# Output projection as a stage of its own between attention and memory queries, by one level of Strassen's algorithm over pairs of token tiles

## Chip, cores and metric

The kernel runs as one program on one core of a Trainium2 chip. The metric is the device time of one execution in microseconds (us). The engines are TensorE (PE; matmuls, and PEld for its weight loads), VectorE (DVE), ScalarE (ACT), GpSimd (POOL) and SyncE (SP), whose queue issues most of the DMA transfers. GpSimd has a DMA queue of its own too (POOLq).

## What is computed

One layer of a streaming encoder over 2048 tokens of 1024 features:

```python
xn = rmsnorm(x, g_mix)
z = xn @ w_in                       # q, k, v (3 x 512), p_in (512), forget logits (8)
fox = forgetting_attention(q, k, v, f_logit)          # 8 heads of 64, causal, (S, 512)
pool = multiscale_pool(p_in, w_pool, pool_scale)      # windows 2, 4, 8, 16, (S, 512)
h = x + concatenate([fox, pool], -1) @ w_out          # w_out 1024 x 1024
mq = rmsnorm per head of (rmsnorm(h, g_mem_q) @ w_mem_q)   # 4 heads of 128
h = h + softmax(mq mk / sqrt(128)) mv @ w_mem_out     # 256 memory tokens
gu = rmsnorm(h, g_ffn) @ w_gate_up
h = h + (silu(gu[:, :2816]) * gu[:, 2816:]) @ w_down
```

All data is float32. A matmul of full precision is made as three in a reduced format (fp32r): each operand is split into a high part (a cast, usually on ScalarE: `act.copy`) and a low part (raw minus high, a subtraction `sub_hi` on VectorE or GpSimd), and `mm3` adds high·high, high·low and low·high into one PSUM bank. So each operand costs a cast and a subtraction, and each product three matmuls.

## The kernel before

Tokens are cut into 16 tiles of 128 (`NT`) or 8 blocks of 256 (`NB`). The stages follow one another on the time line of the profile: memory keys and values and the input projection (0 to 337 us), the pooling stage (337 to 541), the attention (541 to 953), the memory queries (953 to 1316), and the feed-forward part (1316 to 2588), which already uses Strassen's algorithm. TensorE runs in the order in which the program is written in all of these (`in_order`); in the pooling stage the other engines' order is the scheduler's, in the memory queries SyncE's is the program's too.

**Pooling stage.** A loop over blocks n. `project_p` (mm3 of x by the pool columns of the input weights) makes block n's projections in PSUM: 96 matmuls of 128x256, tile `zp`. `x_load`, `x_split` fetch and split a later block of x (raw and low parts take turns in nine places `xl`). `windows(n)` runs on VectorE: it scales out of PSUM into `pT`, makes window sums `s0` to `s3` by doubling, and `mixed`, and splits that into `mxh`, `mxl`. `pooled(n-1)` multiplies by `w_pool` (12 matmuls, tile `op`) and splits the result into `poh`, `pol`. `out_pool(n-2)` multiplies these by the lower 512 rows of `w_out` (`wop`, split on GpSimd at n = 0): 48 matmuls of 128x512 a block (tile `oo`), added to rows of x (`xr`) and written to `h1d`.

**Attention.** A software pipeline of scores and values over heads and blocks. Its result goes, transposed, to DRAM tiles `catT` of 512 tokens. In its tail the upper 512 rows of `w_out` (`wof`, by `load_w_of`) and `w_mem_q` (by `load_w_q`) are loaded and split.

**Memory queries.** A loop over 16 tiles, software-pipelined. `out_fox` multiplies a tile of `catT` (loaded by `load_cat`, split on VectorE) by `wof`, 24 matmuls of 128x512 a tile (tile `mmps`), and adds `h1d`. `query` takes the tile's norm and its transposes `hT`; `query_norm` multiplies by `w_mem_q` and norms each head (ScalarE twice, VectorE, GpSimd three times); `query_t` transposes; `softmax` makes 12 score matmuls of 128x256 (`scps`) and the exponentials; `mem_values` and `mem_out` follow some tiles later. Tiles 0 and 1 are projected ahead of the loop; in iterations n = 0 to 3 `out_fox(n+2)` stands where `mem_out` stands later, and from n = 4 on `out_fox(n+1)` stands between `query_norm` and `query_t`.

Of the kernel before, what the change touches and what calls it, by code (L numbers as in the profile page):

```python
# [16 lines left out]
P = 128  # L17
S = 2048
D = 1024
# [21 lines left out]
def block_kernel(ctx: ExitStack, tc: tile.TileContext, x, xT, memT, cols, rows, w_qkvf, w_p, w_pool, w_out,  # L41
# [9 lines left out]
    def f(ap):  # L51
        return ap.bitcast(F32)
# [54 lines left out]
    catT = [dr.tile([FOXW, 512], F32, name=f"catT{n}") for n in range(4)]  # L107
    h1d = [dr.tile([P, D], F32, name=f"h1d{n}") for n in range(NT)]
# [40 lines left out]
    def x_split(tiles, part=None, qs=range(4)):  # L149

        for q in qs:
# [9 lines left out]
            sub_hi(lo[:], raw[:], hi[:])  # L161
# [27 lines left out]
    with ExitStack() as c0:  # L189
# [120 lines left out]
        with ExitStack() as c1:  # L310
# [65 lines left out]
            def project_p(hs, ls, zs, ks):  # L376

                per = NG // len(zs)
                for k, g in ([(k, g) for k in ks for g in range(NG)] if per == 1 else
                             [(k, g) for g in range(NG) for k in ks]):  # L380
                    mm3(zs[g // per][:, g % per], (wph[k][:, g * P:(g + 1) * P], wpl[k][:, g * P:(g + 1) * P]),
                        (hs[k], ls[k]), k == 0, k == KD - 1)
# [81 lines left out]
    with xstack:  # L464
        wq_ = opened(xstack, "wo_pool", side="right")
# [13 lines left out]
        def stat_bcast(b):  # L479

            diag = xp.tile([P, 2, B], F32, tag="xsq", name="diag", bufs=2)[:, 0].rearrange("p (j t) -> p j t", j=2)
            for j in range(2):
                dve.tensor_scalar(out=diag[:, j], in0=ident[:], scalar1=rstd[:, 2 * b + j:2 * b + j + 1],
                                  scalar2=None, op0=ALU.mult)
            rbp = tpp.tile([P, B], F32, tag="ss", name="rb", bufs=1)
# [5 lines left out]
        def windows(b, zs, rb, prev):  # L491
# [6 lines left out]
            for i, z in enumerate(zs):  # L498
                dve.tensor_tensor(out=pT[:, per * i:per * i + per, HIS:], in0=z[:, :per],
                                  in1=rb.unsqueeze(1).to_broadcast([P, per, B]), op=ALU.mult)  # L500
            cur = pT
            mixed = pt.tile([P, NG, B], F32, tag="mixed", name="mixed")
            for st in range(NG):
                sh = 1 << st
                lead = 2 * sh - 1
                nx = pt.tile([P, NG, HIS + B], F32, tag=f"s{st % 2}", name=f"s{st}")
                dve.tensor_tensor(out=nx[:, st:, lead:], in0=cur[:, st:, lead:],
                                   in1=cur[:, st:, lead - sh:HIS + B - sh], op=ALU.add)
                dve.scalar_tensor_tensor(out=mixed[:, st], in0=nx[:, st, HIS:], scalar=1.0 / (2 * sh),
                                         in1=pT[:, st, HIS:], op0=ALU.mult, op1=ALU.subtract)  # L510
                if b == 0:
                    dve.tensor_tensor(out=mixed[:, st, :HIS], in0=nx[:, st, HIS:2 * HIS], in1=pinv[:, st],
                                      op=ALU.mult)
                    dve.tensor_tensor(out=mixed[:, st, :HIS], in0=mixed[:, st, :HIS], in1=pT[:, st, HIS:2 * HIS],
                                      op=ALU.subtract)
                cur = nx
            mxh = pt.tile([P, NG, B], F32R, tag="mxh", name="mxh")
            mxl = pt.tile([P, NG, B], F32R, tag="mxl", name="mxl")
            act.copy(mxh[:], mixed[:])
            sub_hi(mxl[:], mixed[:], mxh[:])  # L520
            return pT, mxh, mxl

        def pooled(mxh, mxl):
            poh = pt.tile([P, NG, B], F32R, tag="poh", name="poh")
            pol = pt.tile([P, NG, B], F32R, tag="pol", name="pol")
            for i in range(2):
                op = zpp.tile([P, 2, B], F32, tag="z", name="op", bufs=4)
                for j in range(2):
                    g = 2 * i + j
                    mm3(op[:, j], (wph2[:, g], wpl2[:, g]), (mxh[:, g], mxl[:, g]), True, True)  # L530
                for j in range(2):
                    g = 2 * i + j
                    split_gain(poh[:, g], pol[:, g], op[:, j], pscale[:, g:g + 1])
            return poh, pol

        def out_pool(b, poh, pol):
            for j in range(2):
                i = 2 * b + j
                ts = slice(j * P, (j + 1) * P)
                xr = pt.tile([P, D], F32, tag="xr", name="xr", bufs=4)  # L540
                sp.dma_start(xr[:], x[i * P:(i + 1) * P, :])
                for a in range(2):
                    ps = tpp.tile([P, 512], F32, tag="tp", name="oo", bufs=3)
                    for g in range(NG):
                        mm3(ps[:], (poh[:, g, ts], pol[:, g, ts]), (wop[g, a][0][:], wop[g, a][1][:]),
                            g == 0, g == NG - 1)
                    as_ = slice(a * 512, (a + 1) * 512)
                    dve.tensor_tensor(out=xr[:, as_], in0=ps[:], in1=xr[:, as_], op=ALU.add)
                pool.dma_start(h1d[i][:], xr[:])
# [34 lines left out]
        with in_order():  # L584
            prev, mxs, pos, cum = None, {}, {}, cumulated()
            for n in range(NB + 2):
                if n < NB:
                    hs, ls = nxt
                    if n == 0:
                        rb = stat_bcast(0)  # L590
                    else:
                        zs = [zpp.tile([P, 2, B], F32, tag="z", name="zp", bufs=4) for _ in range(2)]
                        project_p(hs, ls, zs, range(KD))
                    if n + 1 < NB:
                        if n > 0:
                            xt = x_load(n + 1)
                        x_split(xt)
                        nxt = x_parts(xt)
                    if n == 0:
                        wop = {}  # L600
                        for g in range(NG):
# [900 lines left out]
```

## Time and profile before

| | us |
|---|---|
| median of three runs | 2611.46 |
| lowest, highest | 2609.98, 2615.81 |
| the profiled execution | 2590.1 |
| its span in the trace | 2588.4 |
| TensorE busy in the span | 2539.1 (98%) |
| VectorE busy | 1700.5 (66%) |
| ScalarE busy | 1247.2 (48%) |
| GpSimd busy | 809.4 (31%) |

The profile is of one execution. Its page gives busy times, the span in 40 equal slices (64.7 us each; a digit is the busy share in tenths, PEclk the clock that TensorE was granted), and the chain of work that ended last. A row of the trace's time line gives start, duration, engine, line, operation, output and inputs, shape, and in brackets how long the engine had been idle before it and what released it. A matmul's duration is longer than the spacing of matmuls that follow one another, so the cost of one is read from starts. A group of instructions is given as busy time and mean ns of one, then the idle time before them and what ended it.

### The profile page before, as it was taken

The numbers are of one execution on the slowest core, as the hardware profiler recorded it, in microseconds if no ns is written. First come the engines' busy times: TensorE is split into PE (matmuls) and PEld (weight loads), VectorE is DVE, ScalarE is ACT, GpSimd is POOL, SyncE is SP. The second block draws the span as 40 slices with busy tenths as digits, with TensorE's granted clock in tenths as the row PEclk, the third lists the DMA queues.
The fourth block names the chain that finished last, engine by engine and source line by source line (L and its number), as shares of the span: only waits on it lengthen the run. The fifth ranks groups of instructions, "written<-read, shape, count | busy, mean of one in ns | idle before, by whom it ended". The sixth has DMA issues, their size and how long they took to land.

```text
span 2588.4 us, 36909 instructions
## 1 busy us (share of the span) xinstructions
PE 2539.1 (98%) x13133; PEld 2181.8 (84%) x13133; DVE 1700.5 (66%) x2933; ACT 1247.2 (48%) x2375; POOL 809.4 (31%) x1087
## 2 busy tenths in 40 slices
PE   8999999999999989999999999999999999999999
PEld 7999989878888868888778888888888888888887
DVE  6444475579889865445687778756766666664554
ACT  6454442158888864444543433334543333333443
POOL 3343230034444442333525455431001122222000
PEclk9999999999999999999999999999999999999999
DMA  6443475346446242222454554447773233334665
GB/s 242 126 133 104 127 221 167 134 134 148 106 119 152 54 134 91 86 86 82 159 207 166 196 187 170 164 159 254 254 268 131 94 125 107 108 116 163 235 208 203
DMA packets 217065, 396.20 MB, mean 153 GB/s; under 512 B 36656, under 2 KB 112176, under 8 KB 206128
## 3 DMA queue, kind: packets, MB, share of 16 engines
q1 hardware_dynamic: 187376, 296.30, 36.3%
q0 software_dynamic: 29504, 97.54, 9.7%
q8 instruction: 103, 1.69, 0.3%
q14 instruction: 82, 0.67, 0.1%
HBM read 268.85 MB, written 124.91 MB: 152 GB/s over the span
## 4 chain that ended last, share of the span: by engine, by line
PE 41%; issue 8%; DVE 1%; POOL 1%; ACT 0%; POOLq 0%; DVEq 0%
PE bk L62 13%; PE bk L60 13%; PE bk L61 13%; DVE ww L55 0%; POOL out_dram L1395 0%; PE mmps L60 0%; PE mmps L62 0%; PE mmps L61 0%; DVE t L966 0%; PE bk L934 0%; POOL xraw L906 0%; DVE cb L55 0%; ACT pm L1068 0%; DVE x22l L55 0%; ACT ww L178 0%
## 5 line engine op out<-in xcount | busy, mean ns | idle before, releaser
L55 DVE TENSOR_TENSOR ww<-draw,ww 128x512 fp32r<-128x512 f32 x308 | 204.4, 702 | 158.0 <-ACT ww L178 157.8
L178 ACT CAST ww<-draw 128x512 fp32r<-128x512 f32 x308 | 179.2, 620 | 221.8 <-PE bk L62 174.2
L55 DVE TENSOR_TENSOR ww<-graw,ww 128x512 fp32r<-128x512 f32 x220 | 178.3, 816 | 107.6 <-ACT ww L178 107.3
L61 PE MATMUL bk<-ww,ww 128*128 128x512 f32 x616 | 239.6, 389 | 0.0
L60 PE MATMUL bk<-ww,ww 128*128 128x512 f32 x616 | 239.6, 389 | 0.0
L62 PE MATMUL bk<-ww,ww 128*128 128x512 f32 x616 | 239.6, 389 | 0.0
L178 ACT CAST ww<-graw 128x512 fp32r<-128x512 f32 x220 | 136.0, 621 | 180.0 <-PE bk L62 160.1
L55 DVE TENSOR_TENSOR pl<-tp,ph 128x512 fp32r<-128x512 f32 (+3 forms) x296 | 176.7, 599 | 32.7 <-ACT ph L781 31.1
L765 PE MATMUL tp<-ident,s 128*128 128x128 f32 x1088 | 174.0, 276 | 8.1 <-DVE pl L55 7.8
L60 PE MATMUL zps<-wh,xhi 128*128 128x386 f32 x512 | 175.7, 343 | 0.1
L702 ACT ACTIVATE s<-s,mx 128x1024 f32<-128x1024 f32 (+2 forms) x192 | 173.8, 906 | 3.8 <-DVE mx L696 1.8
L61 PE MATMUL zps<-wl,xhi 128*128 128x386 f32 x512 | 173.6, 339 | 0.0
L62 PE MATMUL zps<-wh,xl 128*128 128x386 f32 x512 | 173.2, 338 | 0.0
L781 ACT CAST ph<-tp 128x512 fp32r<-128x512 f32 (+3 forms) x296 | 148.7, 514 | 38.8 <-PE tp L765 32.2
L765 PEld LDWEIGHTS tp<-ident,s 128*128 128x128 f32 x1088 | 134.8, 142 | 38.0 <-DVE pl L55 13.5
L750 PE MATMUL acc<-ph,v 128*128 128x512 f32 (+1 forms) x320 | 133.9, 422 | 6.0 <-POOL ph L770 4.9
L62 PE MATMUL bk<-qs,ww 128*128 128x512 f32 x352 | 137.2, 390 | 1.0 <-DVE ww L55 1.0
L60 PE MATMUL bk<-qs,ww 128*128 128x512 f32 x352 | 137.9, 392 | 0.3 <-ACT s L1314 0.3
L61 PE MATMUL bk<-kh,ww 128*128 128x512 f32 x352 | 137.0, 389 | 0.0
L60 PE MATMUL bk<-kl,ww 128*128 128x512 f32 x352 | 136.9, 389 | 0.0
L61 PE MATMUL bk<-cb,ww 128*128 128x512 f32 x352 | 136.9, 389 | 0.0
L62 PE MATMUL bk<-kl,ww 128*128 128x512 f32 x352 | 136.9, 389 | 0.0
(549 smaller groups left out, 7128.3 us busy)
## 6 DMA issues: line engine op xcount, KB each, us to landing
graw<-in_w_gu_dram SPq DMA_DIRECT2D x44, 1024.0 KB, 5.5
draw<-in_w_down_dram SPq DMA_DIRECT2D x66, 256.0 KB, 3.9
xl<-in_xT_dram SPq DMA_DIRECT2D x64, 256.0 KB, 4.8
qkT<-st SPq DMA_DIRECT2D x64, 256.0 KB, 2.7
wdr<-in_w_down_dram SPq DMA_DIRECT2D x22, 512.0 KB, 3.9
vd<-cb SPq DMA_DIRECT2D x16, 512.0 KB, 3.3
xr<-in_x_dram SPq DMA_DIRECT2D x16, 512.0 KB, 3.3
qs<-qkT SPq DMA_DIRECT2D x8, 1024.0 KB, 10.7
```

Source lines behind the costliest of these rows:

```text
L55: (eng or dve).tensor_tensor(out=lo, in0=src, in1=f(hi), op=ALU.subtract)
L60: pe.matmul(ps, lhsT=sh, rhs=mh, start=first, stop=False, skip_group_check=goes_on)
L61: pe.matmul(ps, lhsT=sh, rhs=ml, start=False, stop=False, skip_group_check=goes_on)
L62: pe.matmul(ps, lhsT=sl, rhs=mh, start=False, stop=last, skip_group_check=goes_on)
L178: act.copy(hi, raw)
L702: act.activation(s[:, sl], s[:, sl], AF.Exp, bias=ng, scale=-1.0, accum_out=l[:, q, g:g + 1])
L750: pe.matmul(acc[:, qa * P:], lhsT=v[:, j, :], rhs=pm[:, qa * P:], start=state["n"] == 1, stop=state["n"] == 2 * nk)
L765: pe.transpose(tp[:, q * P:(q + 1) * P], unit["rows"][q][:, j * P:(j + 1) * P], ident[:])
L781: act.copy(ph[:, sl], tp[:, sl])
```

## The change

The output projection is taken out of both stages and made one stage between the attention and the memory queries. For a pair of token tiles (i, i+4) the operand is a 2 by 2 matrix of blocks: x11 and x21 from the attention (`catT`), x12 and x22 from the pooling (now stored as `poolT`), each 128 tokens by 512 features; the weights are b11, b12, b21, b22, the quarters of `w_out`. The seven products of a pair are x11·b11, x12·b21, s2·t2, s1·t1, s3·t3, s4·b22 and x22·t4, where s1 = x21 + x22, s2 = s1 − x11, s3 = x11 − x21, s4 = x12 − s2 and t1 to t4 are sums of the weights. Sums of products gather in three PSUM banks and are added on VectorE to rows of x.

- Pooling stage: `out_pool` is gone. `pooled` scales its result into `po`, which GpSimd's queue writes to `poolT`. `out_sums` makes t1 to t4 from `w_out` (eight calls in all, each two loads of 256 KB, four subtractions of 128x256 on GpSimd, four writes of 128 KB on its queue). The last block's windows are made in two halves.
- Attention's tail: b11 and b21 are loaded and split in place of `wof`, t2 and t1 in place of `w_mem_q`, and the first pair's x11 and x12 are loaded and split.
- New stage: loop over eight pairs. Each loads four parts of 256 KB (the first pair two), makes two sums on VectorE and two on GpSimd, seven splits (ScalarE cast, VectorE subtraction), and 84 matmuls of 128x512; two products of a pair are made during the next. Operands take turns in eleven places. t3, t4 and b22 are loaded at the first pair, `w_mem_q` at the last. Queries 0 to 2, query_norm 0 and 1, and softmax 0 are made at its end.
- Memory queries: the loop starts at n = 2, without `out_fox`; `h1d` is loaded three tiles ahead; `hT` has three places; `w_mem_out` is loaded at the end of n = 2 and 3. `token_ops` subtractions go from GpSimd to VectorE.

```diff
             if n + 1 < NB:
                 if n > 0:
                     xt = x_load(n + 1)
-                x_split(xt)
+                x_split(xt, engs={} if n else {2: pool, 3: pool})
                 nxt = x_parts(xt)
-            if n == 0:
-                wop = {}
-                ...
-                        wop[g, a] = load_split(wq_, w_out[r0:r0 + P, a * 512:(a + 1) * 512], f"wop{g}{a}", pool)
+                diag = stat_diag(n + 1)
...
+            for k in {6: (4, 5), 7: (6, 7)}.get(n, (n - 2,)):
+                if k >= 0:
+                    out_sums(k // 2, k % 2)
-            prev, *mxs[n] = windows(n, zs, rb, prev)
+            prev, mxs[n] = windows(n, zs, rb, prev)
...
-        if n - 2 >= 0:
-            out_pool(n - 2, *pos.pop(n - 2))
-        if 0 <= n - 1 < NB:
-            pos[n - 1] = pooled(*mxs.pop(n - 1))
+        if n > 0:
+            for b in {1: (), 2: (0, 1)}.get(n, (n - 1,)):
+                pooled(b, mxs.pop(b))
...
+def out_sums(k, a):
+    raw = pt.tile([P, 4, B], F32, tag="wor", name="wor", bufs=2)
+    cs = slice(a * B, (a + 1) * B)
+    for c in range(2):
+        r0 = c * FOXW + k * P
+        sp.dma_start(raw[:, 2 * c:2 * c + 2], w_out[r0:r0 + P, :].rearrange("p (a c) -> p a c", a=2)[:, :, cs])
+    b11, b12, b21, b22 = (raw[:, n] for n in range(4))
+    t3 = pt.tile([P, B], F32, tag="wot", name="wot", bufs=2)
+    sub = lambda o, p_, q_: pool.tensor_tensor(out=o, in0=p_, in1=q_, op=ALU.subtract)
+    sub(t3[:], b22, b12)
+    sub(b12, b12, b11)
+    sub(b22, b22, b12)
+    sub(b21, b21, b22)
+    for nm, v in (("t3", t3[:]), ("t1", b12), ("t2", b22), ("t4", b21)):
+        pool.dma_start(osum[nm][:, k, cs], v)
...
+def pair_ops(p_, parts, raw):
+    ...
+    put("x22", x22)
+    tt(x22, x21, x22, ALU.add)
+    tt(x21, x11, x21, ALU.subtract, pool)
+    tt(raw[0], x22, x11, ALU.subtract)
+    put("s2", raw[0])
+    put("s1", x22)
+    put("s3", x21)
+    tt(raw[1], x12, raw[0], ALU.subtract, pool)
+    put("s4", raw[1])
...
+for p_ in range(NP):
+    ...
+    raw = pair_raw(p_)
+    o_ = x_rows(i, 0), x_rows(i, 1, "oh", 2), x_rows(i2, 1)
+    if p_ == 0:
+        out_weights("t3")
+    cur = pair_ops(p_, *raw)
+    if last:
+        queries = [early_query(0)]
+    if p_ == 0:
+        out_weights("t4")
+        out_weights("b22")
+    a, b, c = three_banks(p_, "obk")
+    product_o(a, cur["x11"], "b11", True)
+    o11 = begun(a, i, 0, o_[0])
+    if prev and not last:
+        earlier_1(*prev)
+    product_o(c, cur["x12"], "b21", True)
+    ended(o11, c, i, 0)
+    if last:
+        ...
+        earlier_1(*prev)
+        queries[0]()
+    if prev:
+        earlier_2(*prev)
+    product_o(a, cur["s2"], "t2", False)
+    o12 = begun(a, i, 1, o_[1])
+    product_o(b, cur["s1"], "t1", True)
+    o22 = begun(b, i2, 1, o_[2])
+    product_o(a, cur["s3"], "t3", False)
+    ended(o22, a, i2, 1)
+    prev = cur, (a, b), (i, i2), o12
+...
+queries[1]()
+mqd[0] = query_norm(banks[0], *qd.pop(0))
+earlier_1(*prev)
+mqd[1] = query_norm(banks[0], *qd.pop(1))
+qtd[0] = query_t(mqd.pop(0))
+pmd[0] = softmax([...], pm0, *qtd.pop(0))
+queries[2]()
+earlier_2(*prev)
+qtd[1] = query_t(mqd.pop(1))
...
-    for n in range(NT + 1):
+    for n in range(2, NT + 1):
...
-        if ahead:
-            out_fox(n + 2, 0)
-        elif i < NT:
+        if 0 <= i < NT:
             mem_out(i, h1s[i], mod[i // 2], 0)
```

More of the change, by code (lines that the diff above doesn't have):

```diff
@@ L527, in pooled @@
+            return pT, mx
+        def pooled(b, mx):
+            po = pt.tile([P, NG, B], F32, tag="po", name="po", bufs=2)
+            for i in range(2) if b < NB - 1 else (1, 0):
                 op = zpp.tile([P, 2, B], F32, tag="z", name="op", bufs=4)
@@ L529, in pooled @@
                     g = 2 * i + j
-                    mm3(op[:, j], (wph2[:, g], wpl2[:, g]), (mxh[:, g], mxl[:, g]), True, True)
+                    mm3(op[:, j], (wph2[:, g], wpl2[:, g]), mx[g], True, True)
                 for j in range(2):
                     g = 2 * i + j
[L533 to L549, printed above, removed]
+                    act.activation(po[:, g], op[:, j], AF.Copy, scale=pscale[:, g:g + 1])
+            pool.dma_start(poolT[b // 2][:, b % 2 * B:(b % 2 + 1) * B].rearrange("(g p) t -> p g t", p=P), po[:])
+        def out_sums(k, a):
[13 more added lines that the diff above has]
+                pool.dma_start(osum[nm][:, k, cs], v)
         def cumulated():
```

451 lines of the change are left out of this document (270 added, 181 removed).

## The prediction

> **What bounds the kernel now.** I read the page from the busy times to the slices and the chain, then the waits of the tensor engine, then the stretches around the edited stages.
>
> ```profile
> PE 2539.1 (98%) x13133; PEld 2181.8 (84%) x13133; DVE 1700.5 (66%) x2933; ACT 1247.2 (48%) x2375; POOL 809.4 (31%) x1087
> PE   8999999999999989999999999999999999999999
> DVE  6444475579889865445687778756766666664554
> PEclk9999999999999999999999999999999999999999
> GB/s 242 126 133 104 127 221 167 134 134 148 106 119 152 54 134 91 86 86 82 159 207 166 196 187 170 164 159 254 254 268 131 94 125 107 108 116 163 235 208 203
> PE 41%; issue 8%; DVE 1%; POOL 1%; ACT 0%; POOLq 0%; DVEq 0%
> ```
>
> TensorE is busy 98% of the span, is full in nearly every slice, runs at its full clock and makes up the chain that ended last. VectorE comes near it only in the attention slices (9 to 14). The waits say the same:
>
> ```profile
> PE tp L765 <- DVE pl L55: 7.8, 9, 3.0
> PE acc L750 <- POOL ph L770: 4.9, 3, 3.0
> PE zp L61 <- DVE xl L55: 2.8, 2, 1.9
> PE mmps L60 <- DVE v L646: 1.2, 1, 1.2
> ```
>
> (waited for: total, times, longest). No wait reaches 8 us in all in the stages that are edited. So a matmul taken away is worth its slot on TensorE, and anything added is free until TensorE waits for it. The median of the timed runs, 2611.46 us, stands 0.8% above the profiled execution (span 2588.4, run 2590.1); I work out a difference in the profile's time and subtract it from the median unscaled. A measurement here can tell about 0.2%, 5.2 us, from no change.
>
> **Matmuls removed.** The slot, from starts in the timeline:
>
> ```profile
> 952.97 0.40 PE L60 MATMUL mmps<-qs,v 128*128 128x512 f32 x1
> 958.21 0.39 PE L62 MATMUL mmps<-kh,v 128*128 128x512 f32 x1
> 337.62 0.28 PE L60 MATMUL zp<-xhi,wph 128*128 128x256 f32 x1
> 338.56 0.28 PE L62 MATMUL zp<-xhi,wpl 128*128 128x256 f32 x1
> L60 PE MATMUL oo<-wop00h,poh x16: 389/392/497, 382.3 to 535.4; 128*128 128x512 f32 x16
> L60 PE MATMUL mmps<-qs,v x64: 387/389/499, 953.0 to 1250.0; 128*128 128x512 f32 x64
> ```
>
> The first two rows are the ends of 24 matmuls in a row: (958.21 − 952.97)/23 = 0.228 us a slot of 128x512; the next two, of nine: 0.94/8 = 0.1175 for 128x256. The output projection has 24 groups like oo of 16 and six like mmps of 64: 384 + 384 = 768 matmuls. Strassen needs 8 pairs × 7 products × 4 × 3 = 672. 96 × 0.228 = **21.8 us less**. That count is in the program and can't fail; what can be lost is its cover for others.
>
> **Pooling stage.** It loses 384 × 0.228 = 87.5 us of TensorE work. Does the rest of the stage keep up?
>
> ```profile
> 384.00:500.00 116.00, 116.00 (x762) 106.57 (x761) 68.92 (x127) 24.81 (x46) 5.58 (x10) 1.00 0.45 153
> L548 DVE TENSOR_TENSOR xr<-oo,xr 128x512 f32<-128x512 f32 x20 | 13.7, 686 | 7.9 <-PE oo L62 7.9
> L174 DVE SCALAR_TENSOR_TENSOR pol<-op,colt,poh 128x256 fp32r<-128x256 f32 x20 | 9.2, 480 | 3.5 <-ACT poh L173 3.5
> 404.36 1.77 SPq L145 DMA_DIRECT2D xl<-in_xT_dram  x3
> 406.54 0.69 DVE L55 TENSOR_TENSOR xl<-xl,xhi 128x512 fp32r<-128x512 f32 x1 [4.87 <-PE zp L61]
> 420.13 1.23 DVE L55 TENSOR_TENSOR mxl<-mixed,mxh 128x1024 fp32r<-128x1024 f32 x1 [0.81 <-ACT mxh L519]
> 430.70 0.69 DVE L55 TENSOR_TENSOR xl<-xl,xhi 128x512 fp32r<-128x512 f32 x1 [4.87 <-PE zp L61]
> ```
>
> Between 384 and 500 (PE, PEld, DVE, ACT, POOL busy) TensorE has no gap. A block takes 430.70 − 406.54 = 24.2 us, so the stretch holds 4.8; without its 48 oo matmuls (10.9 us) it has 13.2 us of TensorE work (96 zp and 12 op at 0.1175 are 12.7 of it). VectorE without xr and pol, which go, needs (68.9 − 13.7 − 9.2)/4.8 = 9.6 us of that. By load it fits. By latency it is close: a block's projection ends near 406.5, its windows' last split at 421.4: 14.9 us, less four xr and one pol inside (3.2): 11.7. In the changed order pooled(n) follows project(n+1) and precedes project(n+2), so two blocks take at least 11.7 + 1.4 (op) + 11.3 (zp) = 24.4, or 12.2 each: just inside 13.2. Before, the oo matmuls covered this. What stretches it: three of a block's four x loads are issued only as the projection drains (404.36) and their splits stand in VectorE's queue between the window sums; with the weights' sums they share the queue with four 128 KB writes and two loads more. And GpSimd now makes four subtractions per block:
>
> ```profile
> 368.52 2.30 POOL L55 TENSOR_TENSOR wop20l<-wr,wop20h 128x512 fp32r<-128x512 f32 x1
> 369.62 1.75 DVE L55 TENSOR_TENSOR xl<-xl,xhi 128x512 fp32r<-128x512 f32 x1
> 382.58 0.68 DVE L55 TENSOR_TENSOR xl<-xl,xhi 128x512 fp32r<-128x512 f32 x1
> ```
>
> Beside a GpSimd subtraction a VectorE split took 1.75 us, alone 0.68: 1.07 more. Four collisions make 4.3: chain 16.0, period (16.0 + 12.7)/2 = 14.35, 1.15 over 13.2, for six blocks 6.9 us. With none: 0. The Trainium skill ("SBUF — State Buffer", section "SBUF: two separate sides") calls the pair of ports that the two engines share an exclusive lock: a two-input VectorE operation waits out the whole GpSimd one, so this rule speaks against the sums' place; by its wait alone (half of the 1.28 us of a 128x512 subtraction, four times, 2.6 us) the period would be 13.5 and the cost near 2, an estimate. The trace agrees in kind (0.68 to 1.75). I take 3 from collisions and 2 for the last block, whose windows now stand bare before the attention (two half-chains instead of one behind 48 oo matmuls): **+5**, bounds −3 (the two waits zp on xl go with the eight old wop splits) to +15.
>
> **Start of the new stage.** Its first pair has 24 matmuls ready (5.5 us, to 958.4), then needs s2, from tiles whose loads wait for the attention's last values buffer (953).
>
> ```profile
> v<-catT SPq DMA_DIRECT2D x16, 256.0 KB, 4.0
> 957.02 1.28 POOL L734 TENSOR_TENSOR fo<-fo,lbs 64x512 f32<-64x512 f32 x1 [5.73 <-DMA lbs<-ld]
> 958.60 0.57 POOL L735 DMA_DIRECT2D catT<-fo  x1 [0.29 <-POOL fo L734]
> 959.79 0.50 PE L60 MATMUL mmps<-qs,v 128*128 128x512 f32 x1 [1.19 <-DVE v L646]
> 932.73 0.47 PE L765 MATMUL tp<-ident,s 128*128 128x128 f32 x1 [3.03 <-DVE pl L55]
> 930.00:940.00 10.00, 7.27 (x33) 6.61 (x33) 5.92 (x11) 9.11 (x19) 3.03 (x5) 0.66 0.37 126
> ```
>
> Loads land at about 953.5 + 4.0 = 957.5. s3's subtraction is put on GpSimd behind its last scaling and write (to 959.2), ends near 960.5, and ScalarE casts s3 ahead of s2, which is ready near 961.8: TensorE waits 3.4 us, with 1.2 + 0.4 at the same place before. The t3, t4 and b22 loads (3 MB) and pair 0's rows queue ahead of pair 1: 4.5 MB in the 13.7 us of five products is 330 GB/s, and the best slice shows 268, so up to 3 us more, and I take 2. 3.4 + 2 − 1.6 = **+4**, bounds 0 to +10. The upper end has the clock: after 3.03 us without work at 932.7 it was granted at 0.66 for 10 us, 3.4 us lost if all of it is matmuls. The Trainium skill ("TensorE: Matmul & The Clock Gate", "Part 1: The HAM clock gate") puts the fall at an idle window of about 3.4 us and lets it last about as long: by it this wait stands just at the edge and would lose some 1.7, an estimate; the trace shows a fall after 3.03.
>
> The steady pairs hold: seven products are 84 × 0.228 = 19.1 us, against VectorE's 16 operations (seven splits, two sums, seven sums out of PSUM) × 0.69 = 11.0.
>
> **Query stage.** It loses 87.5 us of fox matmuls, of which the new stage uses 153.2 with the pool half. What they covered:
>
> ```profile
> 973.01 0.69 ACT L1043 ACTIVATE mq<-mmps,hr 128x512 f32<-128x512 f32 x1 [4.61 <-PE mmps L62]
> 976.60 1.04 POOL L1050 TENSOR_TENSOR mq<-mq,r 128x512 f32<-128x512 f32 x1
> 979.10 0.60 PE L871 MATMUL tp<-ident,mq 128*128 128x128 f32 x4
> 980.46 0.75 DVE L877 SCALAR_TENSOR_TENSOR ww<-tp,gqm,ww 128x512 fp32r<-128x512 f32 x1 [0.47 <-ACT ww L876]
> 1195.50:1216.40 20.90, 20.90 (x124) 18.35 (x123) 10.40 (x16) 9.48 (x21) 6.25 (x9) 1.00 0.24 88
> ```
>
> Query norm to scaled query: 973.01 to 977.64, 4.6 us. Transposes to score operand: 979.10 to 981.21, 2.1 us. In the transition query_t(0) stands straight before softmax(0): 2.1 us bare, **+2** (1 to 4). In iterations 2 and 3, which had 24 fox matmuls each and now have no mem_out, only softmax's 12 matmuls (1.4 us) and the transposes of the weights and of the next query (some 1.6 us, an estimate from the 0.60 of four) lie between query_norm and query_t: 1.6 us each bare, and some for the turned tiles: **+4** (2 to 9). Later a tile takes 20.9 − 24 × 0.228 = 15.4 us of TensorE, more than VectorE's 10.4, and mem_out covers the 4.6: 0. The attention keeps its eight weight splits in its tail: 0.
>
> **Sum.** −21.8 + 5 + 4 + 2 + 4 = −6.8: profiled run 2583.3, median 2611.46 − 6.8 = **2604.7 us**.
>
> **Rivals.**
> *Slower: the pooling stage becomes bound by its VectorE–GpSimd chain.* For: the 10.9 us cover goes, and collisions cost 1.07 each. Against: 9.6 us of load in 13.2, and ScalarE and GpSimd little used there (24.8 and 5.6 of 116). It decides from the period where six blocks eat 21.8 − 10 (start, transition, loop) = 11.8 us: 13.2 + 2.0 = 15.2. If x loads also land 2 us later and the sums meet VectorE six times a block (6.4), the chain is 20.1 and the period 16.4: 6 × 3.2 = 19.2, so −21.8 + 19.2 + 10 = +7.4: 2618.9; with eight meetings 2625.
> *No change: the new seams take the gain.* The start at its upper bound (10), the loop at its (9), transition 2 : −21.8 + 5 + 10 + 2 + 9 = +4; with one of the two only, −2: 2610.
> *The whole gain.* Work on TensorE is reordered around each chain; if all seams hide but the 2.1: −21.8 + 2 = −19.8: 2591.7.
>
> **Chances.** Forecast 0.45, whole gain 0.15, no change 0.21, slower 0.19. Beyond 5.2 us faster: the whole gain and 0.42 of the forecast, 0.57; slower: its rival and 0.01 of the seams', 0.20; within: 0.23. The range, 2590 to 2621, goes from the whole gain to the slower rival with six to seven meetings.
>
> **What would show it.** Right: 672 matmuls at 0.228 in the new stage; a zp period of 13.2 to 14.4 us; one TensorE wait of 3 to 4 us after its first 24 matmuls, on s2's split; two waits near 1.6 us before the transposed queries. Wrong: a zp period of 15 us or more with op waiting on mxl; a granted clock under 0.9 over the new stage; waits of TensorE on DMA in every pair.

## The result, and the profile after

The changed kernel takes 2626.91 us (median of six runs, 2624.12 to 2631.64), the one before 2610.72 (2608.52 to 2615.81): 16.2 us slower, ratio 1.0062 with a 95% interval of 1.0046 to 1.0077. The forecast was 2604.7 in a range of 2590 to 2621: wrong in its sign, and out of its range by 6 us. The profiled execution of after took 2625.6 us. Later runs were made on several chips, on which the kernel before has medians from 2589 to 2621 us, so ratios to before on the same chip are compared and not times.

The page after, busy times, slices and chain:

```profile
PE 2534.1 (97%) x13037; PEld 2175.6 (83%) x13037; DVE 1740.7 (66%) x2955; ACT 1285.1 (49%) x2444; POOL 880.8 (34%) x1185
PE   8999989899999799899999999999999999999998
PEclk9999999999999899999999999999999999999999
PE 47%; issue 8%; DVE 2%; ACT 1%; DMA 1%; POOL 1%; SPq 0%; POOLq 0%; DVEq 0%; ACTq 0%
```

TensorE has 96 records fewer and only 5 us less busy time, in a span 35 us longer than the 2588.4 of the first profile of before. Its waits (total, times, longest):

```profile
PE tp L791 <- DVE pl L55: 14.9, 7, 6.5
PE acc L776 <- POOL ph L796: 10.6, 5, 3.0
PE obk L60 <- DVE o L1178: 7.7, 4, 3.3
PE obk L60 <- ACT ww L181: 5.2, 1, 5.2
PE tp L891 <- POOL mq L1071: 3.6, 2, 2.0
PE rb L491 <- DVE diag L484: 3.3, 1, 3.3
PE obk L62 <- DVE ww L55: 1.7, 1, 1.7
```

The obk rows are the new stage's, and they are new; the first two are the attention's, twice what they were in the first profile of before. To tell what belongs to the change, both kernels were profiled three times (the last pair on one chip). Stage lengths from the starts of matmuls, us:

| | before | after | before, less or plus the moved matmuls |
|---|---|---|---|
| first projection of the pooling stage to first score | 203.7, 204.0, 203.8 | 121.0, 123.3, 126.1 | 203.7 − 87.5 = 116.2 |
| first score to last value matmul | 411.9, 423.5, 408.9 | 434.1, 418.0, 413.4 | as before |
| from there to the feed-forward part's first bank | 366.7, 366.2, 366.7 | 458.3, 451.4, 456.3 | 366.7 + 153.2 − 87.5 = 432.4 |
| feed-forward part | 1263.3, 1263.2, 1263.2 | 1263.2, 1264.3, 1264.2 | as before |
| last matmul to the end of the span | 5.6, 5.6, 5.8 | 9.9, 9.9, 9.9 | as before |

The matmuls fell by 21.8 us as counted. Against that stand 5 to 10 us in the pooling stage, 19 to 26 in the new stage and the memory queries together, 4.3 at the end, and in the attention 4.5 on the same chip (413.4 against 408.9). The last pair of spans differs by 21.1 us, and the rows of the table sum to that: −77.7 + 4.5 + 89.6 + 1.0 + 4.1 = 21.5, with 0.4 less ahead of them.

**The new stage.** Its first pair in the time line, and a window with the busy times of PE, PEld, DVE, ACT and POOL, the granted clock and the DMA:

```profile
900.35 3.38 POOL L1144 TENSOR_TENSOR praw<-v,praw 128x512 f32<-128x512 f32 x2 [1.32 <-DVE praw L1144]
900.85 0.68 DVE L1178 TENSOR_TENSOR o<-obk,o 128x512 f32<-128x512 f32 x1
902.09 1.14 ACT L181 CAST ww<-praw 128x512 fp32r<-128x512 f32 x2 [1.23 <-POOL praw L1144]
903.28 0.80 PE L60 MATMUL obk<-qs,ww 128*128 128x512 f32 x1 [5.16 <-ACT ww L181]
903.88 0.63 PE L61 MATMUL obk<-kl,ww 128*128 128x512 f32 x1
907.91 0.47 PE L61 MATMUL obk<-kl,ww 128*128 128x512 f32 x1
916.17 0.50 PE L62 MATMUL obk<-qs,ww 128*128 128x512 f32 x1 [1.66 <-DVE ww L55]
901.25:908.08 6.83, 4.80 (x11) 3.48 (x12) 5.38 (x8) 5.46 (x11) 4.05 (x4) 0.50 1.02 402
```

The first 24 matmuls end at 898.1 and s2 comes at 903.3, with ScalarE's cast of s3, which waits for GpSimd, ahead of s2's: the mechanism that the prediction gave, 5.2 us instead of 3.4. Afterwards ten matmuls take 4.6 us (903.28 to 907.91) where 2.3 are usual: 2.3 us more to the lower clock, which the window shows granted at 0.50 from 901.25 to 908.08. The Trainium skill ("TensorE: Matmul & The Clock Gate", "Part 1: The HAM clock gate") has half the rate after an idle window of some 3.4 us; the rate agrees, but here it fell 3.1 us behind the end of the last matmul, and it lasted 6.8 us. Then, which the prediction did not have, the last product of the second pair (rows of SyncE's queue first):

```profile
919.32 15.60 SPq L1173 DMA_DIRECT2D o<-in_x_dram  x4
935.00 0.38 SPq L652 DMA_DIRECT2D praw<-catT  x1
931.40 0.69 DVE L1144 TENSOR_TENSOR praw<-praw 128x512 f32<-128x512 f32 x1 [0.81 <-POOL praw L1144]
932.01 2.96 DVE L55 TENSOR_TENSOR ww<-praw,ww 128x512 fp32r<-128x512 f32 x3
934.88 1.27 DVE L1178 TENSOR_TENSOR o<-obk,o 128x512 f32<-128x512 f32 x2
935.62 0.80 PE L60 MATMUL obk<-ot,ww 128*128 128x512 f32 x1 [3.29 <-DVE o L1178]
```

The product s3·t3 goes on in the bank that holds x11·b11 + s2·t2, so it must wait until VectorE has added that bank to a row of x (o, L1178). VectorE came to it only after a wait for GpSimd's sum and three splits of later operands (0.99 us each beside GpSimd's next sum, 0.69 usual). For the pairs that follow SyncE's queue counts too: it stood 15.6 us at four row loads, with the operands of a coming pair behind them. Four such waits make the 7.7 us. Around two of them the clock was at half again (935.4 to 938.8 and 1058.3 to 1061.7), another 3.3 us lost. With that the stage adds up: 150.2 us of matmuls at their usual spacing and transposes, 14.5 of waits (6.8 at the first two, 7.7 at the four) and 5.6 at half the clock are 170.3, and it took 170.4.

**Memory queries.** From the first query norm to the feed-forward part after took 287.9, 286.2 and 287.8 us; 432.4 less 150.2 for what comes before (648 products × 0.228 and 2.4 of transposes) would be 282.2. The waits are where they were expected:

```profile
1078.09 0.39 PE L60 MATMUL qbk<-ww,ww 128*128 128x256 f32 x1 [0.97 <-ACT ww L896]
1094.68 0.66 PE L891 MATMUL tp<-ident,mq 128*128 128x128 f32 x4 [1.64 <-POOL mq L1071]
1105.95 1.07 PE L891 MATMUL tp<-ident,mq 128*128 128x128 f32 x4 [1.97 <-POOL mq L1071]
```

**Attention.** Two waits at its start that before has at 0.6 us at most:

```profile
462.92 0.75 POOL L546 DMA_DIRECT2D poolT<-po  x1 [3.26 <-ACT po L545]
464.34 0.69 DVE L717 CUSTOM_DVE_ANT_0 s<-sps,cm 128x512 f32<-128x512 f32 x1 [2.47 <-POOL cm L706]
465.09 0.50 PE L715 MATMUL sps<-kh,qs 128*128 128x512 f32 x1 [2.19 <-DVE mx L717]
455.48 0.34 SPq L459 DMA_DIRECT2D qs<-qkT  x1
487.82 1.25 POOL L760 TENSOR_TENSOR fo<-fo,lbs 64x512 f32<-64x512 f32 x1 [9.04 <-DMA lbs<-ld]
490.07 0.33 PE L791 MATMUL tp<-ident,s 128*128 128x128 f32 x1 [3.51 <-DVE pl L55]
```

The same places before:

```profile
518.16 0.42 SPq L456 DMA_DIRECT2D qs<-qkT  x1
546.22 0.44 PE L689 MATMUL sps<-kh,qs 128*128 128x384 f32 x1 [0.62 <-DVE mx L691]
562.90 0.66 PE L765 MATMUL tp<-ident,s 128*128 128x128 f32 x4 [0.43 <-DVE pl L55]
```

The last write of the pooling result stands in GpSimd's queue for ScalarE's scaling, and the causal masks (cm) of the first scores stand behind it: 2.2 us in every profile with that write in that queue. And the first head's loads begin at 455, as the last projection ends, 3 us ahead of the first score (before: at 518, 23 us ahead, beside the oo matmuls); the small load of factors (lbs) comes behind them, and GpSimd waits 9 us for it.

### The profile page after: what moved, and what is told of

Its sections match the earlier page's. It is cut to its first block, busy times and chain, and to the rows that moved or that the text cites. A ratio compares the mean times of both kernels' runs of the same rounds, so it can differ in the third digit from the quotient of the medians.

```text
span 2623.8 us, 37146 instructions
## 1 busy us (share of the span) xinstructions
PE 2534.1 (97%) x13037; PEld 2175.6 (83%) x13037; DVE 1740.7 (66%) x2955; ACT 1285.1 (49%) x2444; POOL 880.8 (34%) x1185
## 3 DMA queue, kind: packets, MB, share of 16 engines
q0 software_dynamic: 32448, 105.93, 10.5%
## 4 chain that ended last, share of the span: by engine, by line
PE 47%; issue 8%; DVE 2%; ACT 1%; DMA 1%; POOL 1%; SPq 0%; POOLq 0%; DVEq 0%; ACTq 0%
PE bk L62 13%; PE bk L60 13%; PE bk L61 13%; PE mmps L60 2%; PE mmps L62 2%; PE mmps L61 2%; PE tp L891 1%; DMA wqr<-in_w_mem_q_dram 0%; DVE ww L55 0%; POOL out_dram L1573 0%; ACT mq L1064 0%; DVE ms L1068 0%; PE mops L62 0%; PE mops L61 0%; PE mops L60 0%
## 5 line engine op out<-in xcount | busy, mean ns | idle before, releaser
L1573 POOL DMA_DIRECT2D out_dram<-o x32 | 17.3, 541 | 382.6 <-DVE o L1570 381.6
L60 PE MATMUL bk<-kl,ww 128*128 128x512 f32 x352 | 136.9, 389 | 0.0
```

What stands on the lines that cost most here:

```text
L60: pe.matmul(ps, lhsT=sh, rhs=mh, start=first, stop=False, skip_group_check=goes_on)
L1573: pool.dma_start(out[rows_, cs], o)
```

## The experiments

Theories: (1) the loss in the new stage is an order of queues: VectorE and ScalarE stand at GpSimd's sums, or SyncE's queue at rows of x; (2) the attention is slower; (3) the pooling stage loses to GpSimd's subtractions.

**a0_before, g3_before, g4_after, a1_after** (no edit).

> The kernel before, unchanged, profiled a second time. The profiled execution of before (2590.1 us) lies some 20 us under the median of its timed runs (2610.7), and the profiled one of after (2625.6) lies at its median. Theory A (the attention is slowed by the change, 434 us from first score to last value matmul against 412): this profile shows 411 to 415 us of attention again. Theory B (the attention's length varies from run to run in both kernels, and the first profile of before was a short one): 420 to 433 us of attention here, run at 2605 to 2615 us, and the change's real loss outside the pooling stage is the waits in the new stage and behind it, about 26 us.

Measured: run 2602.4 us, attention 423.5. Theory B holds for the attention (the run is somewhat faster than its 2605 to 2615): the first profile of before was short. Its waits of TensorE at head changes show how (time line; compare 3.03 us at most in the first profile):

```profile
661.28 0.38 PE L750 MATMUL acc<-ph,v 128*128 128x256 f32 x1 [2.48 <-POOL ph L770]
714.24 0.58 PE L750 MATMUL acc<-ph,v 128*128 128x256 f32 x1 [4.47 <-POOL ph L770]
```

The clock goes with them: TensorE was granted half the clock for 20.5 us of this attention and for 10.2 us of the first one. So the doubled waits of the attention in the first comparison were no work of the change, except those at its start.

> The changed kernel, unchanged, beside the experiments on one chip. Expected ratio to before 1.006, as measured. In the profile: from the last value matmul of the attention to the first query norm 170 us, of which 150 are matmuls at 0.228 and transposes (648 products x 0.228 + 2.4), so 20 us of waits and of lower clock; from the query norm to the feed-forward part 288 us against 282 by the prediction's sum without waits; from first score to last value matmul 424 to 434.

Measured: ratio 1.0063 (1.0046 to 1.0080); stage (from the last value matmul to the first query norm) 165.3 against 170.4 in the first profile, memory queries 286.2, attention 418.0.

> The kernel before, for its attention on one chip with the next: from first score to last value matmul 412 to 424 us in two profiles so far.

> The changed kernel on the same chip. By the accounts of the other stages (pooling -81, new stage and memory queries +85 to +92, end +4.3, against a measured +16) its attention should be 3 to 8 us longer than before's here; theory: 2.2 us of it at the masks behind the last pooling write, 1 to 4 at the first head's factors behind the head's loads, the rest in the tail. Rival (the attention is not touched): within 3 us of before's.

Measured on that one chip: 408.9 and 413.4, 4.5 us more, in the range of the theory. The 2.2 us and 1.4 us at the start are in g4's rows and not in g3's: waits over 0.25 us come to 5.7 us in the first 40 us of g4's attention and to 1.6 in g3's, and to 13.5 and 13.7 in the rest, and both had half the clock for 10.2 us. So the start makes nearly all of the 4.5; the tail, of which the theory had a part, makes none. It is one profile of each.

**e1_sums_dve**

```diff
-            tt(x21, x11, x21, ALU.subtract, pool)
+            tt(x21, x11, x21, ALU.subtract)
-            tt(raw[1], x12, raw[0], ALU.subtract, pool)
+            tt(raw[1], x12, raw[0], ALU.subtract)
```

> The changed kernel with the two pair sums that GpSimd makes (s3 and s4's raw sums) made on VectorE. Theory 1 (VectorE and ScalarE stand in their queues behind GpSimd's sums, and TensorE's banks come free late: waits of 7.7 us on the sums out of PSUM and 6.8 at the first pair's s2): the waits fall to 2 to 5 us in all, the kernel is 8 to 14 us faster than the changed one, at 2613 to 2619 us. Theory 2 (the operands themselves arrive late, because SyncE's queue stands at row loads ahead of the next pair's operands): the waits stay, time within 3 us of the changed kernel's 2626.9. Either way VectorE has 18 x 0.69 = 12.4 us of work in a pair of 19.1.

Measured: ratio 1.0048 (1.0036 to 1.0060), 0.0014 or some 4 us under the changed kernel's, with intervals that overlap; theory 1 had 8 to 14. Stage 162.4 us against 165 to 170. All waits on L1178 are gone. The start grew worse:

```profile
904.39 0.76 PE L60 MATMUL obk<-qs,ww 128*128 128x512 f32 x1 [6.44 <-ACT ot L181]
918.27 0.80 PE L62 MATMUL obk<-qs,ww 128*128 128x512 f32 x1 [3.29 <-DVE ww L55]
```

**e2_raw_first**

```diff
-    raw = pair_raw(p_)
+    raw = raws.pop(p_)
+    if 0 < p_ < NP - 1:
+        raws[p_ + 1] = pair_raw(p_ + 1)
     o_ = x_rows(i, 0), x_rows(i, 1, "oh", 2), x_rows(i2, 1)
```

> The changed kernel with the loads of the next pair's operands issued ahead of this pair's rows of x, from pair 1 on (SyncE runs in the written order; in the changed kernel four row loads stood 15.6 and 12.2 us at their places, with the next operands behind them). Theory 2: the waits on the sums out of PSUM at pairs 2, 5, 6, 7 (3.3, 1.3, 0.4, 2.7 us) go, and the clock dip after the first with them: 8 to 12 us faster than the changed kernel, 2615 to 2619. Theory 1 (GpSimd's sums): the waits stay within 2 us of those, time 2623 to 2628.

Measured: ratio 1.0048 (1.0036 to 1.0060), again some 4 us where the theory had 8 to 12; stage 163.4 us. The waits of pairs 5 to 7 (counted from 0) are gone, those of pair 1 are not (0.9 and 2.3 us). So both theories were half right: the bank's sum is late when VectorE's operands are late and also when GpSimd slows them; of the 7.7 us of waits one edit takes out all, the other more than half.

**e5_both, f0_both_again** (both edits)

> Both edits at once: pair sums on VectorE, and the next pair's operands loaded ahead of this pair's rows. Theory (either of them alone lets VectorE reach the sums out of PSUM in time, so they are two ways to remove the same wait): the gain over the changed kernel is hardly more than one alone, ratio to before 1.003 to 1.0045. Rival (they are separate losses that add): 1.002 or less. The wait for the first pair's s2 stays at 4.6 to 6.5 us in both.

> The kernel with both edits (pair sums on VectorE, next operands ahead of the rows), unchanged, beside the next one on one chip: ratio to before 1.002 to 1.005, 160 us from the attention's last value matmul to the first query norm.

Measured: 1.0034 (1.0020 to 1.0048) and 1.0035 (1.0023 to 1.0047), stage 160.0 and 159.9: in the theory's range, though the gain is twice that of one edit; the intervals are too wide to tell two ways from two losses. Of the stage's 15 to 20 us over 150.2, 10 remain, at the first pair's s2 and at the second's x11. The releaser at s2 was in one profile the bank's sum:

```profile
893.87 0.76 PE L60 MATMUL obk<-qs,ww 128*128 128x512 f32 x1 [5.54 <-DVE o L1178]
907.75 0.50 PE L62 MATMUL obk<-qs,ww 128*128 128x512 f32 x1 [2.26 <-DVE ww L55]
```

**e4_no_pool_subs**

```diff
-            sub(t3[:], b22, b12)
-            sub(b12, b12, b11)
-            sub(b22, b22, b12)
-            sub(b21, b21, b22)
-            for nm, v in (("t3", t3[:]), ("t1", b12), ("t2", b22), ("t4", b21)):
+            for nm, v in (("t3", b11), ("t1", b12), ("t2", b22), ("t4", b21)):
```

> The changed kernel without the 32 subtractions of the weights' sums in the pooling stage: the raw quarters are written in their place, so loads and writes stay and only GpSimd's work is left out (the sums of the weights are not made). The prediction put 3 us on their collisions with VectorE: from first projection to first score 118 us against 121.0, and 2622 to 2625 us in all. Rival (the stage is held by the latency of loads and window sums, not by GpSimd): 120.5 to 121.5 us, time the same. Rival (the exclusive port holds VectorE for much more): under 116.5 us, 5 us or more faster.

Measured: ratio 1.0062 (1.0049 to 1.0074), pooling stage 122.4 us, between the 121.0 to 126.1 with the sums. No cost of GpSimd's subtractions to the pooling stage can be seen; with 5 us between profiles of one kernel, and VectorE's order there left to the scheduler (TensorE's waits moved from the first diagonal to the windows' products, 2.0 and 3.7 us), the 3 us of the prediction are not excluded. The port rule of the Trainium skill ("SBUF — State Buffer", "SBUF: two separate sides"), by which the prediction had some 2 us, shows in single rows here; what it decided stands in the new stage (f2 and g1 below).

**e6_s2_first, e7_pool_sp**

(on top of both edits)

```diff
+            tt(raw[0], x22, x11, ALU.subtract)
+            put("s2", raw[0])
+            put("s1", x22)
             tt(x21, x11, x21, ALU.subtract)
-            tt(raw[0], x22, x11, ALU.subtract)
-            put("s2", raw[0])
-            put("s1", x22)
             put("s3", x21)
...
+                cur = pair_ops(p_, *raw)
                 if p_ == 0:
                     out_weights("t3")
-                cur = pair_ops(p_, *raw)
...
-            pool.dma_start(poolT[b // 2][...], po[:])              # e7 alone
+            (sp if b == NB - 1 else pool).dma_start(poolT[b // 2][...], po[:])
```

(From the second pair on s3 is made from the place that s2's sum has taken, so its values are others; the instructions are the same.)

> Both edits, and in pair_ops s2 and s1 are made and split ahead of s3, and the split of t3 behind the first pair's operands. Theory (the first pair's s2 is late because ScalarE's queue holds other casts ahead of it: s3's behind GpSimd in the changed kernel, t3's with the sums on VectorE): the wait falls from 5.2 (6.4 with the sums on VectorE) to 3 to 3.5 us and the clock keeps nearer 1; 2 to 4 us faster than with both edits alone. Rival (the operands x21 and x22 land too late whatever the order): the wait stays over 4.6 us, time the same within 1.5 us.

Measured: 1.0031 (1.0020 to 1.0043), stage 160.2; the wait stayed at 5.85 us, as the rival has it, but it does not end with the operands' landing. In the time line VectorE's sum out of the first bank comes last, behind s3's and s4's sums:

```profile
885.71 0.68 DVE L1178 TENSOR_TENSOR o<-obk,o 128x512 f32<-128x512 f32 x1
886.54 0.77 PE L60 MATMUL obk<-qs,ww 128*128 128x512 f32 x1 [5.85 <-ACT ww L181]
```

TensorE starts 0.15 us behind that sum's end (886.39); the releaser named is another.

> As the one with s2 first, and the last block's write of the pooling result is put on SyncE's queue instead of GpSimd's. In the changed kernel every profile has a wait of 2.2 us of TensorE some 7 us after the first score: VectorE waits for masks that GpSimd makes behind that write, which waits for ScalarE's last scaling. Theory: that wait goes (under 0.8 us), 1 to 2.5 us off the attention's start. Rival (the mask is late because TensorE's own order puts the last op matmuls there): it stays near 2 us.

Measured: 1.0053 (1.0035 to 1.0070), no gain over e6. The wait at the masks went from 2.2 to 0.5 us as the theory said, and one place on it came back:

```profile
466.50 0.39 PE L715 MATMUL sps<-kh,qs 128*128 128x256 f32 x1 [0.53 <-DVE mx L717]
489.69 0.47 PE L791 MATMUL tp<-ident,s 128*128 128x128 f32 x1 [6.03 <-DVE pl L55]
```

The attention, reached earlier, waits for the first factors instead (6.0 us against 0.8 to 4.6 in the other kernels): that load then sets its start.

**f1_dve_order** (VectorE's order in pairs 0 to 6 written by hand: each sum out of PSUM right behind its product, the next pair's splits between; shortened, and the remarks behind # are not in the code)

```diff
-        with in_order(EN.SP):
+        with in_order(EN.SP, EN.DVE):
...
             product_o(a, cur["x11"], "b11", True)
             o11 = begun(a, i, 0, o_[0])
+            step()          # this pair's s1, s3 and the sum for s4
...
             product_o(c, cur["x12"], "b21", True)
             ended(o11, c, i, 0)
+            step(p_ + 1)    # the next pair's x11, x12; then x22, s2 behind the next products
```

> Both edits, and VectorE's order in pairs 0 to 6 written by hand: each sum out of PSUM right behind the product that ends it, the operands of the next pair spread between them, operands two pairs ahead in SyncE's queue, and at the first pair x11's sum out of PSUM ahead of s2's split. With the s2-first edit the wait at the first s2 product stayed at 5.9 us and ended with VectorE's sum out of the bank that the product goes on in. Theory (the bank is read late, because VectorE's queue has operands ahead of it): the first wait falls from 5.6 to 3 to 4 us, what is left being the landing of x21 and x22 and the chain of sums behind them, the second (x11 of pair 1) goes or falls below 1 us, and the stage takes 153 to 157 us; ratio to before 1.001 to 1.0025. Rival (the operands' landing sets it): the stage stays at 159 to 161 us, ratio as with both edits.

Measured: 1.0056 (1.0042 to 1.0070), stage 163.9 where the theory had 153 to 157.

```profile
886.32 0.47 PE L60 MATMUL obk<-qs,ww 128*128 128x512 f32 x1 [2.60 <-ACT ww L181]
903.18 0.79 PE L60 MATMUL obk<-qs,ww 128*128 128x512 f32 x1 [4.58 <-ACT ww L181]
```

The first wait fell to 2.6 us, which bears out that the bank's late sum had held it (casts and loads were moved too, so it does not show that alone); what it gained was lost at pair 1, where ScalarE had stood 7.4 us at the casts of t4, whose loads were now behind pair 1's.

**f2_weights_last, f3_diag_first** (on top of f1; shortened)

```diff
-                open_pair(1)
-                for nm in ("t4", "b22"): ...
+                for w_ in (w3, *w4b): next(w_)     # loads of t3, t4, b22
+                open_pair(1)                       # loads of pair 1; splits of t4, b22 later
...
+                diag = stat_diag(n + 1)            # f3 alone
                 x_split(xt, engs={} if n else {2: pool, 3: pool})
-                diag = stat_diag(n + 1)
```

> The kernel with VectorE's order by hand, with three things changed at the first pair: t4 and b22 are loaded ahead of pair 1's operands (their places are free while the operands wait for theirs), split behind pair 1's x11 and x12 in the program, and the two sums that hold the place of pair 1's operands are made ahead of s1's split. With the hand order the first wait fell from 5.5 to 2.6 us, but x11 of pair 1 was then 4.6 us late. Theory (that wait came from ScalarE's casts of t4, which stood for their late load ahead of x11's cast): it falls under 2.5 us, the stage takes 156 to 160 us against 163.9 and 159.9; ratio to before 1.002 to 1.0035. Rival (some 4.5 MB must land within the first five products whatever their order): the sum of the first pair's waits stays at 7 to 9 us and the stage over 160.

Measured: 1.0039 (1.0027 to 1.0050), stage 165.5, so the rival by its time, but not by its reason:

```profile
919.45 0.77 PE L60 MATMUL obk<-qs,ww 128*128 128x512 f32 x1 [4.52 <-ACT ww L181]
935.25 0.80 PE L61 MATMUL obk<-ot,ww 128*128 128x512 f32 x1 [7.10 <-DVE ot L55]
928.57 8.43 DVE L55 TENSOR_TENSOR ot<-wor,ot 128x512 fp32r<-128x512 f32 x4
924.74 5.02 POOL L55 TENSOR_TENSOR ot<-ww,ot 128x512 fp32r<-128x512 f32 x4
929.73 4.92 POOL L55 TENSOR_TENSOR ob<-ww,ob 128x512 fp32r<-128x512 f32 x4
```

TensorE waits for VectorE's splits of t3, whose casts ScalarE had ended at 924.0, so this wait is for no load. The first of the four took 6.63 us (0.68 usual): it stood until GpSimd's eight splits of t4 and b22, which follow one another without a gap, had ended at 934.6. In the kernel with both edits the second wait is of this kind too: VectorE's split of the second pair's x11 took 2.26 us (e5) and 2.01 (f0) beside GpSimd's of b22, and TensorE waited 2.5 and 2.3 us for it.

> As f2, and in the pooling stage the two diagonals of a block's statistics are made ahead of its splits of x. In every profile of the changed kernel TensorE waits 3.3 to 3.9 us for the first diagonal near 370 us, where VectorE is 98% busy. Theory (the statistics stand behind x's splits in VectorE's queue): that wait goes, the pooling stage takes 118 to 120 us against 121 to 123; ratio to before 0.0008 to 0.0015 under f2's. Rival (VectorE has more work there than the blocks' projections cover, so the wait moves to a projection that needs x's splits): 121 to 123 us.

Measured: 1.0047 (1.0035 to 1.0059), not under f2's; pooling stage 122.7 (120.1 in f2). The rival holds by its time: the wait near 370 is gone, and 4.15 us stand at a later diagonal, not at a projection.

```profile
403.92 1.22 PE L491 MATMUL rb<-diag,ones 128*128 128x256 f32 x2 [4.15 <-DVE fe L590]
```

**g1_no_burst**

```diff
-                sp.dma_start(r, ...)           # t3, t4, b22
+                pool.memset(r, 0.0)
```

> The kernel with both edits, with t3, t4 and b22 set to zero by GpSimd in place of their six loads (3 MB) at the first pair (so four of the seven products' weights are kept); their splits stay. Theory (the first pair's waits come from 4.5 MB that must land in five products): the second wait (2.3 to 2.5 us, at pair 1) goes and the first falls below 4 us, the stage takes 153 to 156 us against 160, ratio to before 1.001 to 1.002. Rival (the chain from x21 and x22 through sums, casts and the sum out of PSUM is long by itself): the first wait stays over 5 us, the stage over 157.

Measured: 1.0055 (1.0038 to 1.0071), stage 166.9, and the first wait is 15.5 us. The edit changed more than the burst: without loads to wait for, the splits of t3 came ahead of the first pair's operands. They took VectorE 2.5 us; then the first of three splits of the pair's operands took 8.03 us (0.69 usual) beside six splits of GpSimd without a gap:

```profile
885.00:895.00 10.00, 0.00 (x0) 0.00 (x0) 10.00 (x5) 4.13 (x8) 9.02 (x8) 0.57 0.00 0
886.54 9.23 DVE L55 TENSOR_TENSOR ww<-praw,ww 128x512 fp32r<-128x512 f32 x3
886.66 4.93 POOL L55 TENSOR_TENSOR ot<-ww,ot 128x512 fp32r<-128x512 f32 x4
891.55 2.47 POOL L55 TENSOR_TENSOR ob<-ww,ob 128x512 fp32r<-128x512 f32 x2
```

The two make 9.8 us of the 10 by which the first wait grew over both edits' 5.5 and 5.6. On the burst the run is inconclusive: the second wait fell from 2.3 or 2.5 to 0.6 us, but most of GpSimd's splits, which had held it, were done by then too.

**g2_sp_writes, g5_best** (both edits; the same kernel twice)

```diff
-                pool.dma_start(osum[nm][:, k, cs], v)
+                sp.dma_start(osum[nm][:, k, cs], v)
-            pool.dma_start(poolT[b // 2][...], po[:])
+            sp.dma_start(poolT[b // 2][...], po[:])
```

> The kernel with both edits, with the writes of the weights' sums and of the pooling result on SyncE's queue instead of GpSimd's. From the start of the last matmuls to the end of the span: 9.9 us with the change, 5.6 before. Theory (something at the program's end goes with the number of transfers on GpSimd's queue): it falls to under 8. Rival (it does not hang on that queue): 9.8 to 9.9. What it does to the pooling stage is not forecast: SyncE's queue then waits for GpSimd's sums between x's loads.

> The kernel with both edits and the two kinds of writes on SyncE's queue, timed. If the 4.0 us at the end of the span are time of the program, the ratio to before falls from 1.0034 (both edits) to 1.0015 to 1.0025; if they are only records of the profile, it stays at 1.003 to 1.004. Faster than before is not expected: what is left are the first pair (8 us), the attention (4.5), the memory queries' seams (5) and the pooling stage (4 to 7) against 21.8.

Measured: the end of the span 5.9 us behind the last matmul in both, so the theory holds and 4.0 us are back; the pooling stage 119.9 and 118.0. The ratio of g5 is 1.0035 (1.0022 to 1.0048), as with both edits and not the 1.0015 to 1.0025 of its forecast. As in e7, the attention, reached earlier, then waits for the first factors: 6.0 and 6.1 us of TensorE behind GpSimd, which waits for them. No version was faster than before; the fastest stand at 1.0031 to 1.0035.

## Why the prediction was wrong, point by point

- **Matmuls removed** (−21.8): right. 672 in the new stage, at 0.228 us where nothing waits.
- **Pooling stage** (+5): near, 4.8, 7.1 and 9.9 us over 116.2 in three profiles, but for another reason. Collisions with GpSimd, put at 3, showed no cost (e4); one of the sums' subtractions took 0.75 us, and the 1.28 that the prediction halved is of a 64x512 operation. The period of the late blocks was as forecast (14.5 and 13.2 us from 431 on). What waits are a block's statistics and the decay sums on VectorE, early in the stage; after f3's edit took one wait away the next came, which speaks for VectorE having no room there but was not tested further.
- **Start of the new stage** (+4, bounds 0 to 10): 5.2 + 1.7 of waits and 2.3 of clock, less 1.6: 7.6, inside the bounds. The path by s3's cast ahead of s2's was there; a second path, the first bank's sum on VectorE, held it as soon as the first was opened (e6, f1). The 2 us for a burst of loads are not shown: the wait at the second pair's x11 was one for VectorE's split beside GpSimd's splits of b22 (f2, g1).
- **"The steady pairs hold"** (0): the step that failed most. It compared VectorE's load, 11.0 us, with 19.1 of matmuls. The load fits; the order does not. Banks are read in VectorE's queue behind the next operands, those stand behind GpSimd's sums, and the operands' loads behind row loads. That cost 7.7 us of waits and 3.3 of lower clock, 11.0 where the sum had 0; the new stage was 15 to 20 us over its matmuls in all, and both edits together took 5 to 10 of them back (e5).
- **Transition and loop** (+2 and +4): right together, 1.3 and 3.6 us of waits, and 4.0 to 5.7 us by the stage's length.
- **Attention** (0): wrong, 4.5 us on one chip, 4.1 of them at its start. The prediction looked at the tail's splits and not at what its start had been covered by: the masks behind a write in GpSimd's queue, and the first head's loads, which the oo matmuls had hidden.
- **End of the span** (not in the sum): 4.3 us.
- **Rivals.** The slower case came true with another mechanism than the one named. The seams of "no change", which had 0.21, are nearer: its sum with the start at 7.6, the steady pairs' 11.0, the attention's 4.5 and the end's 4.3 comes to −21.8 + 7 + 7.6 + 11 + 5 + 4.5 + 4.3 = +17.6, against 16.2 measured. The terms are of profiles that differ by some us, so that it comes this near is in part luck.

What stays open: how much of the first wait the landing of x21 and x22 sets, and how much the chain of sums behind them; what the stage takes with the splits of t4 and b22 off GpSimd, which no run tried; and why the end hangs on GpSimd's queue.

## What to carry to other kernels

Matmuls that are taken away were also cover. For each stage from which they go, list what stood behind them: the loads that began under them, the writes in each queue, the sums that read a bank; an engine's load against TensorE's time says nothing of that. Where a product goes on in a bank that another engine must first read, a late read stops TensorE: put right behind the product it took the wait from 5.5 to 2.6 us here (f1), and the stage gained nothing, since the operands and loads around it came late instead. Work given to GpSimd in one run can hold a single VectorE subtraction for the whole run (6.6 and 8.0 us for 0.7), so it should not stand where VectorE has operands due. Profile both kernels on one chip before a stage's difference is put down to the change.

## What was not expected of the hardware

The end of the span lay 9.8 or 9.9 us behind the last matmul in every kernel with the sums' 32 writes on GpSimd's queue (32448 packets on it in the changed kernel against 29504 before), and 5.9 when these and the 8 of the pooling result went to SyncE's queue (29760). None of the kernel's work stands there, but the trace has a drain instruction of GpSimd at the program's end: 7.66 us in the changed kernel, 3.43 before, 3.73 with the writes moved. The length of the attention, unchanged code, ran from 409 to 423 us in three profiles of before, with the waits for a small load of factors at head changes between 0.5 and 4.5 us. The clock was granted at half in spells of 3.4 or 6.8 us, and not behind long waits alone: in g3 from 709.9 to 713.3 us behind a wait of 1.5. One VectorE subtraction stood for 8.03 us beside six of GpSimd that followed one another.
